# A hybrid attention, Fourier and feed-forward layer on one core: attention's tiles placed in another order, the first feed-forward weights split into attention's buffers, and the start of the second sequence issued in another order

## The chip, the cores and the metric

The kernel runs on one core of a Trainium2 chip. The metric is the time of one execution on the device in microseconds (us), the median of several runs. The core has a tensor engine for matmuls (PE, with its weight loads listed apart as PEld), a vector engine (DVE), a scalar engine (ACT), GpSimd (POOL), a sync engine that issues DMAs (SP), two on-chip memories (SBUF, and PSUM with eight banks, into which PE writes) and 16 DMA engines. Each engine takes its instructions in the order of its own queue, and an instruction that has to wait holds up those behind it.

## The reference

One encoder layer for two sequences of 1024 rows of width 1024, all in float32, with a conditioning vector of their own each. `g_final` is the final norm's gain.

```python
def layer(x, c, ...):
    sh1, sc1, ga1, sh2, sc2, ga2 = split(silu(c) @ w_ada + b_ada, 6)
    h = rmsnorm(x, g_mix) * (1 + sc1) + sh1
    q_lat, kv_lat, k_pe, f_in = split(h @ w_in)
    y_mla = mla_group(...)        # attention with low-rank q and k/v, 4 heads
    y_four = fourier_group(...)   # real part of a 2-D Fourier transform, mixed by group
    x = x + ga1 * (concat(y_mla, y_four) @ w_out)
    h2 = rmsnorm(x, g_ffn) * (1 + sc2) + sh2
    return x + ga2 * ((silu(h2 @ w_gate) * (h2 @ w_up)) @ w_down)
# both sequences go through layer(), then rmsnorm(x, g_final)
```

## The kernel before, in words

**Precision.** Every large matmul is done as three: an operand is split into a high part (a cast on ACT, line L62) and a low part (a subtraction on DVE, L63, which needs the cast), and `mm3` (L78 to L80) adds high x high, high x low and low x high into one PSUM bank. `split(hi, lo, src)` makes such a pair and keeps the two instructions in `here["a"]` and `here["v"]`.

**Stages.** One after the other: input projections; the Fourier part; attention (two sequences of four blocks of four heads, two tiles of 128 rows each: 64 items `k`); the output projection, which runs some items behind attention; the feed-forward's up stage (gate and up) and down stage for sequence 1 (`s == 0` in the code), then for sequence 2 (`s == 1`).

**Attention's tiles.** The pool `e` ("p3e", left side of SBUF) holds what attention reads: the query weights `wq_h` and `wq_l`, two small buffers `hv`, the rotation tables `rc` and `rs`, the keys `lat0`, the query tiles `qsk`, `qa`, `qp`, the latents `ql`, the values `ckv` and the gates `gah`. `stage3_loads` creates them, and tiles lie in the order of their first creation; `q_tiles` creates `qsk`, `qa` and `qp` ahead of `ql` and `ckv`, and an empty tile of 32 bytes ("phase") follows. The pool `w` ("p3", right side) holds `p` (softmax results), `lat1` and the flipped results `pt`. `scores` reads `qa`, `qp` and the keys; `flip_p` transposes and splits `p` into `pt` one item later; `values` multiplies `pt` with `ckv` three items later, and its split goes into the tiles `o0` and `o1` of the pool `tl` ("p4").

**From attention to the feed-forward.** The pool `w` of the feed-forward ("p5") starts at the address at which `e` started, and its tiles (H20, X0, X1, H21, H30, H31, H41, H00, H01, H50 and so on, 8 KB each) lie again in order of creation. A tile can be written as soon as the last reader of every older tile under it is done. `prep_h` loads and splits the seven combinations of the activations that the feed-forward multiplies (a fast matrix product with 7 in place of 8 block products), two half tiles at each `next(prep)`. The first two are ordered behind the last split of `flip_p`; the sums of the first weights (`w0`, four subtractions on DVE) are ordered behind the split of the last `values`; some of norm2 and of the residual adds (L883) are ordered behind the splits (`first(...)`). The last four output projections of sequence 2 (`out_proj(1, 3, ...)`) close the pool `tl`; the pool "p5b" (`wh`, `wl`, `val`) then takes its place.

**The up stage.** For each of 22 weight columns `n` seven products, `step(0)` to `step(6)`, each of twelve matmuls into the banks x, y, z. `combos(n + 1)` loads the next weights (`rgu`) and forms their four sums (`sums_w`, L135) on POOL; after each product one of the next seven weight tiles is split (`hl`). After product 0, ACT copies x into `p1` (L1351); product 2 accumulates further on x. After product 1, DVE adds y and `p1` into `u2` (L138); product 3 accumulates further on y. In the same way the adds after products 3, 4 and 5.

**Row steps.** The down stage's last result is finished row tile by row tile (`rows_out`): a product with the gate (L1467), an add, a square on ACT (L1469), a reciprocal root on POOL (L105 to L110), two scalings on DVE (L1478) and two stores by SP (L1484). For sequence 1 these seven steps stand in the list `pending` and are issued in the first iterations of sequence 2's up stage, two in each: one behind the copy of `p1` and one behind the Silu after product 2, by `behind()` ordered behind the last split on ACT and on DVE.

**What sets the order.** The program's text does not fix the queues. A planner walks through it with estimated durations and takes for each engine the earliest instruction of the program that is ready at that moment. `tc.issue_after(i)` puts every instruction of the block on `i`'s engine behind `i`; it is an order of issue only.

## Time and profile before

| | us |
|---|---|
| median of three runs | 2081.8 |
| lowest, highest | 2078.99, 2082.57 |
| the profiled execution | 2080.45 |
| its span, first to last instruction | 2078.6 |
| mean granted clock of PE | 0.987 |

| stretch of the span, us | what runs |
|---|---|
| 0 to 238 | input projections |
| 238 to 331 | Fourier part |
| 331 to 784 | attention and output projections |
| 784 to 1427 | feed-forward of sequence 1 |
| 1427 to 2079 | feed-forward of sequence 2 |

A row of a profile names a line of the kernel, an engine, an operation and the tiles that it writes and reads (out<-in). In the timeline the first column is the start in us from the span's start, the second the length, and a bracket gives how long the engine stood idle before and what ended that. In the list of waits a row gives who waited, for whom, the total in us, the number of times and the longest. The windows view gives for each stretch the busy time of each engine with the number of its instructions, then the granted clock of PE as a share of full speed, the DMA's share and its rate. Matmuls overlap, so the length of one (0.39 us for 512 columns) is more than the distance between two starts.

### The profile page before, as it was taken

To read this page: it belongs to the slowest core of one execution; us is meant where nothing else is said; L and a number is where in the kernel's file an instruction comes from. 1 tells how busy PE (TensorE), PEld (TensorE's weight loads), DVE (VectorE), ACT (ScalarE), POOL (GpSimd) and SP (SyncE) were. 2 spreads that over 40 slices of the span, in tenths; PEclk is the share of its full clock that TensorE was granted. 3 is DMA by queue.
4 is the path that set the end of the run, shared out by engine and by line. 5 is a ranking of instruction groups with operands and counts; after the bars stand their busy time and mean duration, and the time that the engine had idled before them with its cause. 6 is when DMAs were issued, how large, how long until landed. Compare 5 with 4: busy or idle time off the path is not lost. (4 is left out here: it accounts for less than half of the span.)

```text
span 2078.6 us, 28790 instructions
## 1 busy us (share of the span) xinstructions
PE 2008.3 (97%) x10044; PEld 1667.0 (80%) x10044; DVE 1413.0 (68%) x2089; ACT 903.1 (43%) x1765; POOL 837.3 (40%) x1034
## 2 busy tenths in 40 slices
PE   5899999999999999999999999999999999999997
PEld 2788877888888877888888888877788888888876
DVE  2757757766676768887778776777765565567684
ACT  2666535555565545333333356453333333336441
POOL 1455203111312314888778610335544454420142
PEclk7999999999999999999999999999999999999999
DMA  9586774544543456555555587664332232258672
GB/s 372 191 252 198 230 273 176 132 102 90 149 122 112 155 195 208 176 194 183 192 187 190 165 277 265 212 233 158 136 116 99 89 127 101 78 183 281 221 232 90
DMA packets 182943, 371.30 MB, mean 179 GB/s; under 512 B 19021, under 2 KB 58317, under 8 KB 179725
## 3 DMA queue, kind: packets, MB, share of 16 engines
q1 hardware_dynamic: 163660, 309.80, 44.6%
q0 software_dynamic: 19136, 59.65, 9.5%
q8 instruction: 79, 1.29, 0.3%
q14 instruction: 68, 0.55, 0.1%
HBM read 257.38 MB, written 120.39 MB: 182 GB/s over the span
## 5 line engine op out<-in xcount | busy, mean ns | idle before, releaser
L78 PE MATMUL bank<-H,wh 128*128 128x512 f32 x1232 | 482.2, 392 | 9.7 <-DVE val L138 5.0
L80 PE MATMUL bank<-H,wl 128*128 128x512 f32 x1232 | 481.4, 391 | 1.4 <-DVE wl L63 1.4
L79 PE MATMUL bank<-H,wh 128*128 128x512 f32 x1232 | 481.9, 391 | 0.4 <-DVE H L63 0.4
L138 DVE TENSOR_TENSOR val<-bank,val 128x512 f32<-128x512 f32 x244 | 166.8, 688 | 182.6 <-PE bank L80 179.4
L78 PEld LDWEIGHTS bank<-H,wh 128*128 128x128 f32 x1232 | 232.7, 189 | 60.6 <-DVE val L138 6.1
L80 PEld LDWEIGHTS bank<-H,wl 128*128 128x128 f32 x1232 | 232.7, 189 | 50.5 <-DVE wl L63 1.9
L79 PEld LDWEIGHTS bank<-H,wh 128*128 128x128 f32 x1232 | 232.6, 189 | 49.0 <-DVE H L63 0.8
L63 DVE TENSOR_TENSOR wl<-draw,wh 128x512 fp32r<-128x512 f32 x286 | 201.2, 738 | 87.8 <-ACT wh L62 86.1
L62 ACT CAST wh<-draw 128x512 fp32r<-128x512 f32 x286 | 168.9, 620 | 159.3 <-PE bank L79 81.0
L79 PE MATMUL bank<-wl,wh 128*128 128x512 f32 x572 | 223.9, 391 | 1.9 <-DVE wl L63 1.9
L138 POOL TENSOR_TENSOR val<-val 128x512 f32<-128x512 f32 x58 | 82.9, 1437 | 352.1 <-DVE val L1452 189.4
L78 PE MATMUL bank<-wh 128*128 128x512 f32 x572 | 222.7, 389 | 0.2 <-ACT wh L62 0.2
L80 PE MATMUL bank<-wh,wl 128*128 128x512 f32 x572 | 222.7, 389 | 0.0
L62 ACT CAST wh<-rgu 128x512 fp32r<-128x512 f32 x172 | 107.0, 622 | 261.3 <-PE bank L79 207.3
L62 ACT CAST wh<-val 128x512 fp32r<-128x512 f32 x133 | 82.3, 622 | 270.0 <-PE bank L79 245.1
L63 DVE TENSOR_TENSOR wl<-val,wh 128x512 fp32r<-128x512 f32 x133 | 143.1, 1078 | 68.4 <-ACT wh L62 68.2
L63 DVE TENSOR_TENSOR wl<-rgu,wh 128x512 fp32r<-128x512 f32 x172 | 165.8, 964 | 4.3 <-ACT wh L62 4.3
L135 POOL TENSOR_TENSOR val<-rgu 128x512 f32<-128x512 f32 x84 | 120.3, 1432 | 117.3 <-DMA rgu<-in_wgu_dram 108.3
L79 PEld LDWEIGHTS bank<-wl,wh 128*128 128x128 f32 x572 | 107.3, 188 | 27.8 <-DVE wl L63 5.7
L78 PEld LDWEIGHTS bank<-wh 128*128 128x128 f32 x572 | 107.4, 188 | 23.1 <-ACT wh L62 0.7
L80 PEld LDWEIGHTS bank<-wh,wl 128*128 128x128 f32 x572 | 107.4, 188 | 22.0
L950 DVE TENSOR_REDUCE mx<-ps_s 128x1 f32<-128x1024 f32 x64 | 78.2, 1222 | 62.3 <-PE ps_s L945 61.9
(362 smaller groups left out, 4107.2 us busy)
## 6 DMA issues: line engine op xcount, KB each, us to landing
rgu<-in_wgu_dram SPq DMA_DIRECT2D x86, 512.0 KB
draw<-s_d SPq DMA_DIRECT2D x143, 256.0 KB
s_d<-val POOLq DMA_DIRECT2D x88, 256.0 KB, 4.0
draw<-t_d SPq DMA_DIRECT2D x88, 256.0 KB
s_d<-val SPq DMA_DIRECT2D x66, 256.0 KB
draw<-in_w_down_dram SPq DMA_DIRECT2D x55, 256.0 KB
wada<-in_w_ada_dram SPq DMA_DIRECT2D x13, 1024.0 KB
xt<-in_x_dram SPq DMA_DIRECT2D x16, 512.0 KB
```

The source lines that it names most:

```text
L62: here["a"] = nc.scalar.copy(hi, src).ins
L63: here["v"] = nc.vector.tensor_tensor(out=lo, in0=src, in1=rd(hi), op=ALU.subtract).ins
L78: nc.tensor.matmul(out, lh, rh, start=first, stop=False, skip_group_check=cont)
L79: nc.tensor.matmul(out, lh, rl, start=False, stop=False, skip_group_check=cont)
L80: nc.tensor.matmul(out, ll, rh, start=False, stop=last, skip_group_check=cont)
L135: return eng.tensor_tensor(out=out, in0=x, in1=y, op=ALU.subtract).ins
L138: eng.tensor_tensor(out=out, in0=x, in1=y, op=ALU.add)
L950: nc.vector.tensor_reduce(out=mx, in_=ps, axis=AX.X, op=ALU.max)
```

## The change

- **Attention's pools.** `q_tiles` is gone. `stage3_loads` creates `qsk`, then `ql` and the values' tiles, then `qa`; `qp` is created at its first use, after `ckv`. The empty tile of 32 bytes is left out. In "p3" an empty tile of 32 bytes is created in front of `pt` and one of 480 bytes behind it.
- **First weights.** The first two weight tiles of sequence 1's up stage are split in the third of the last four output projections, into a tile each of the tags `o0` and `o1` of the pool `tl` (high and low parts). The up stage reads them from there, and splits the third tile on as before.
- **First sums of sequence 2.** `combos` forms the sums of iteration 0's and iteration 1's weights of sequence 2 on DVE.
- **The copy and the second split.** In both sequences the split after product 1 is ordered on ACT behind the copy of `p1`.
- **Row steps.** The pending steps are issued behind the adds after products 1 and 3, on DVE's queue alone, in place of the two places above. `add` returns its instruction for that.

```diff
     def add(out, x, y, eng):
-        eng.tensor_tensor(out=out, in0=x, in1=y, op=ALU.add)
+        return eng.tensor_tensor(out=out, in0=x, in1=y, op=ALU.add).ins
...
-    def q_tiles():
-        sk_tile()
-        qa_tiles()
-        qp_tile()
...
         lat = [e.tile([P, 2, N], F32R, tag=f"lat0{i}", name=f"lat0{i}") for i in range(2)]
-        q_tiles()
-        e.tile([P, 8], F32, name="phase")
+        sk_tile()
         load_q(0, 0)
...
             split(wq_h[:, c, 0:512], wq_l[:, c, 0:512], wqr[:, 0:512])
+        qa_tiles()
         nc.sync.dma_start(rc, a["ropec"])
...
         def flip_p(s, b, h, u):
             p = S.pop(("p", s, b, h, u))
+            if (s, b, h, u) == (0, 0, 0, 0):
+                w.tile([P, 8], F32, name="phase_pt")
             if u == 0:
                 S["pt", s, b, h] = [w.tile([P, 8, 2, P], F32R, tag=f"pt{k}", name=f"pt{k}", bufs=2) for k in range(2)]
+            if (s, b, h, u) == (0, 0, 0, 0):
+                w.tile([P, 120], F32, name="phase_l")
...
             if n == 1:
                 norm3(0)
+            if n == 2:
+                fw = [tl.tile([P, 2, 512], F32R, tag=f"o{i}", name=f"fw{i}", bufs=3) for i in range(2)]
+                for i in range(2):
+                    split(fw[0][:, i, :], fw[1][:, i, :], w0[i])
...
-                return sums_w([...], lambda i: val(), nc.gpsimd)
+                return sums_w([...], lambda i: val(), nc.vector if n == 0 or (s == 1 and n == 1) else nc.gpsimd)
...
             if s == 0:
-                wts = [hl(w0[i]) for i in range(2)]
+                wts = [(fw[0][:, i, :], fw[1][:, i, :]) for i in range(2)]
+                fw = None
...
                     elif src is not None:
-                        nxt.append(hl(src[j]))
+                        with ExitStack() as after:
+                            if j == 1:
+                                after.enter_context(tc.issue_after(here["p1"]))
+                            nxt.append(hl(src[j]))
...
                 p1 = val()
-                nc.scalar.copy(p1, x)
-                if pending:
-                    with behind():
-                        pending.pop(0)()
+                here["p1"] = nc.scalar.copy(p1, x).ins
                 step(1, y, 5, True)
                 u2 = val()
-                add(u2, y, p1, nc.vector)
+                here["u"] = add(u2, y, p1, nc.vector)
+                if pending:
+                    with tc.issue_after(here["u"]):
+                        pending.pop(0)()
                 step(2, x, 1, False)
                 sg = val()
                 nc.scalar.activation(sg, x, AF.Silu)
-                if pending:
-                    with behind():
-                        pending.pop(0)()
                 step(3, y, 6, False)
                 u3 = val()
-                add(u3, y, p1, nc.vector)
+                here["u"] = add(u3, y, p1, nc.vector)
+                if pending:
+                    with tc.issue_after(here["u"]):
+                        pending.pop(0)()
```

More of the change, by code (lines that the diff above doesn't have):

```diff
@@ L1245, in combos @@
                     nc.sync.dma_start(r[:, i, :], a["wgu"][i, f])
-                return sums_w([r[:, 0, :512], r[:, 0, 512:], r[:, 1, :512], r[:, 1, 512:]], lambda i: val(), nc.gpsimd)
+                return sums_w([r[:, 0, :512], r[:, 0, 512:], r[:, 1, :512], r[:, 1, 512:]], lambda i: val(), nc.vector if n == 0 or (s == 1 and n == 1) else nc.gpsimd)
             def comb_h(s, c):
```

## The prediction

> **What bounds the kernel now.** I read the page first (busy time by engine), then who the tensor engine (PE) waited for in three stretches, then the timeline round each long wait.

> ```profile
> PE 2008.3 (97%) x10044; PEld 1667.0 (80%) x10044; DVE 1413.0 (68%) x2089; ACT 903.1 (43%) x1765; POOL 837.3 (40%) x1034
> ```

> The change removes no matmul, so at most the 70.3 us of the span (2078.6 less 2008.3) in which PE stands still can go, and with them the time in which it runs slowly after standing still. Who it waited for from 745 to 860 us (attention's end and the feed-forward's start) and from 1420 to 1500 (sequence 2's start), in total us, times, longest:

> ```profile
> PE gb L78 <- DVE x L883: 4.0, 1, 4.0
> PE bank L78 <- DVE val L138: 2.3, 2, 2.1
> PE bank L80 <- DVE wl L63: 1.4, 1, 1.4
> PE bank L78 <- ACT val L1351: 1.3, 1, 1.3
> ...
> PE bank L78 <- ACT wh L62: 0.3, 1, 0.3
> ```

> ```profile
> PE bank L78 <- ACT val L1351: 3.1, 1, 3.1
> PE bank L78 <- DVE val L138: 2.8, 1, 2.8
> ```

> The windows view, cut at the moments when the granted clock falls; columns: stretch, length, PE busy (matmuls), weight loads, DVE, ACT, POOL, then PE clock:

> ```profile
> 765.80:769.20 3.40, 3.40 (x9) 2.63 (x9) 2.41 (x5) 0.81 (x1) 0.64 (x4) 0.50 0.92 303
> 799.90:803.30 3.40, 3.40 (x10) 2.65 (x9) 3.40 (x5) 0.00 (x0) 0.00 (x0) 0.50 0.00 0
> 838.60:842.00 3.40, 3.40 (x15) 2.83 (x16) 2.37 (x3) 1.04 (x3) 3.08 (x4) 1.00 0.05 19
> 1434.80:1441.60 6.80, 5.73 (x14) 4.47 (x15) 6.10 (x9) 2.67 (x6) 2.30 (x3) 0.50 0.43 155
> 1482.60:1486.00 3.40, 3.40 (x9) 2.62 (x9) 3.40 (x3) 0.00 (x0) 3.24 (x3) 0.50 0.01 4
> ```

> After waits of 4.0, 2.1, 3.1 and 2.8 us the clock is 0.50 for 3.4 us (6.8 once); after the one of 1.3 it stays at 1.00. So a long wait costs itself and half of the PE time at half clock: 1.7 us, and 2.9 (half of 5.73) at 1434.8. A 512-column matmul takes 3.40/15 = 0.227 us at full clock, a block of twelve 2.72.

> [...]

> **The change part by part**

> *Attention's pool.* In KB from the pool's start, tiles lie in order of first use: wq 0-12, hv, rc, rs to 20, lat0 20-36, qsk 36-40, then before qa 40-46, qp 46-54, ql 54-62, ckv 62-70, gah 70-72; after ql 40-48, ckv 48-56, qa 56-62, qp 62-70, gah. The feed-forward's pool starts at the same address: H30 32-40, H31 40-48, H41 48-56, H00 56-64, H01 64-72. So H00 and H01, the first split activations, lie before on ql and ckv, and after on qa, qp and gah. ckv is read until attention's last value product; qa and qp only until its last scores. H41 (the sums of the first weights) gets ckv instead, but those sums are already ordered behind that product's split. H31 gets ql in place of qa and half of qp, so SP issues its loads some steps earlier; nothing waits for them. ACT, then DVE:

> ```profile
> 753.23 0.37 ACT L62 CAST o0b<-gb 128x256 fp32r<-128x256 f32 x1 [1.61 <-PE gb L80]
> 761.42 1.99 ACT L62 CAST H<-H 128x1024 fp32r<-128x1024 f32 x2 [7.82 <-PE gb L79]
> ```

> ```profile
> 762.50 2.36 DVE L63 TENSOR_TENSOR H<-H,H 128x1024 fp32r<-128x1024 f32 x2 [5.84 <-ACT H L62]
> 764.78 0.68 DVE L883 TENSOR_TENSOR x<-x,gb 128x512 f32<-128x512 f32 x1
> ```

> ACT stands at the cast of H for 7.8 us until PE has done the value product (761.4); DVE stands 5.8 behind it; the next output projection's residual add (L883) is queued behind both, and PE's bank behind that add: the wait of 4.0. After, both halves of the split (1.99 and 2.36) fit into ACT's and DVE's idle time from 753 on. Gone: 4.0 + 1.7. Late next: norm2 of the last of these rows, which PE's transposes need.

> ```profile
> 767.73 0.68 DVE L135 TENSOR_TENSOR H<-rgu 128x512 f32<-128x512 f32 x1
> ...
> 770.51 0.68 DVE L883 TENSOR_TENSOR x<-x,gb 128x512 f32<-128x512 f32 x1
> ...
> 775.33 0.75 DVE L896 TENSOR_SCALAR xn<-x,rs_r 128x1024 f32<-128x1024 f32 x1 [1.27 <-POOL rs_r L110]
> ```

> Value product ends 761.4, its split 0.37 + 0.42 with hand-overs 762.3, four weight sums (767.73 to 770.5, 2.8) 765.1, the add 765.8, then as in the trace 4.9 from the add's end (771.2) to the scaled row's (776.1): 770.7. PE has three blocks (8.2) until 769.6. It waits 1.1, where the trace has 0.4 at this place: I take 0.8 back. **Gain 4.9**; bounds 3 (the chain 2 later) and 5.7.

> The two empty tiles (32 and 480 bytes) and the 32 bytes taken out move pt, ql and ckv by small offsets. No row shows an offset's price; two rows of the value products, one shape on differently placed tiles:

> ```profile
> L78 PE MATMUL gb<-pt,ckv 128*128 128x256 f32 x256 | 73.7, 288 | 0.0
> ...
> L79 PE MATMUL gb<-pt,ckv 128*128 128x256 f32 x256 | 72.8, 284 | 0.0
> ```

> 0.9 us between them, three such lines: 2.7 either way at most; I take 0. At attention's start nothing is won: in the PE waits from 100 to 745 us no wait names wq or ql.

> *First weights in attention buffers.* The first two weight tiles are split into o0/o1 slots, free since an earlier projection, instead of wh/wl slots that lie on wv and wait for the last projection. Gone: 1.4 (L80 on wl) and 0.3 (wh). The two casts and subtractions move ahead, into DVE's idle time (3.35 before 782.30). Late next is the add at 798.83, the wait of 2.1:

> ```profile
> 782.30 0.75 DVE L1156 TENSOR_SCALAR X<-x,rs_r 128x1024 f32<-128x1024 f32 x1 [3.35 <-POOL rs_r L110]
> ...
> 792.60 1.77 DVE L1156 TENSOR_SCALAR X<-X,rs_r 128x1024 f32<-128x1024 f32 x1 [1.87 <-POOL rs_r L110]
> ...
> 798.83 0.68 DVE L138 TENSOR_TENSOR val<-bank,val 128x512 f32<-128x512 f32 x1
> ```

> Ahead of it DVE waits 1.87 on POOL's reciprocal root of a square on ACT; with two casts fewer (about 0.5 each) that square comes 1.0 sooner. So 1.0 of the 1.7 is kept. **Gain 1.0**; bounds 0 and 5.5 (1.7, and 2.1 + 1.7 if DVE takes the add before the splits of H that stand in front of it).

> *Copy of the first product ahead of the second weight's cast* (j == 1):

> ```profile
> 837.40 0.62 ACT L62 CAST wh<-val 128x512 fp32r<-128x512 f32 x1 [5.10 <-POOL val L135]
> 837.93 0.58 ACT L1351 COPY val<-bank 128x512 f32<-128x512 f32 x1
> ```

> ACT stood 5.1 us at a cast that needs POOL's sum, with the copy behind it; PE's third product accumulates on the bank that is copied. In the new order the copy runs when the first product is done; the cast, late anyway, is needed an iteration later. **Gain 1.2** of the 1.3.

> *Sequence 2's first sums on DVE, same order.* The same cast, here with the copy right behind it, then POOL's sums and DVE's splits:

> ```profile
> 1434.72 0.62 ACT L62 CAST wh<-val 128x512 fp32r<-128x512 f32 x1 [2.69 <-POOL val L135]
> ```

> ```profile
> 1424.20 1.29 POOL L135 TENSOR_TENSOR val<-rgu 128x512 f32<-128x512 f32 x1 [13.35 <-DMA rgu<-in_wgu_dram]
> ...
> 1434.76 1.60 POOL L135 TENSOR_TENSOR val<-rgu,val 128x512 f32<-128x512 f32 x1
> ```

> ```profile
> 1430.08 1.79 DVE L63 TENSOR_TENSOR wl<-rgu,wh 128x512 fp32r<-128x512 f32 x1
> ...
> 1436.83 1.28 DVE L63 TENSOR_TENSOR wl<-rgu,wh 128x512 fp32r<-128x512 f32 x2
> ```

> Eight POOL sums (1424.2 to 1436.4) become eight on DVE at 0.7. While POOL sums, a DVE split takes 1.79; when it stops, 0.64: what the sums add (5.6) the splits give back. From the weights' landing: four sums to 1427.0, eight splits at 0.64 to 1432.1, four sums to 1434.9, then the add that the fourth product needs, done 1435.6; that product is due three blocks after the first, 1435.87 - 3.10 - 5.44 + 8.16 = 1435.5. Gone 3.1 + 2.9, back about 0.4. **Gain 5.6**; bounds 0 and 6.0.

> *Row steps behind the adds:*

> ```profile
> 1473.61 3.62 DVE L1375 TENSOR_TENSOR val<-val 128x512 f32<-128x512 f32 x1
> 1477.16 2.44 DVE L1478 SCALAR_TENSOR_TENSOR val<-val,rs_r,gf 128x512 f32<-128x512 f32 x2
> 1479.52 2.24 DVE L63 TENSOR_TENSOR wl<-val,wh 128x512 fp32r<-128x512 f32 x1
> 1481.68 0.68 DVE L138 TENSOR_TENSOR val<-bank,val 128x512 f32<-128x512 f32 x1
> ```

> Two row scalings (2.44) and a split stand ahead of the add on which PE waits 2.8. After, the scalings are queued behind the add, and the add is ready before the split's cast has come: it runs at 1477.2, ahead of PE's 1479.65. Queued behind it: scalings, split, and the output stores on SP, which nobody waits for. **Gain 4.5**; bounds 0 and 4.5.

> Sum 4.9 + 1.0 + 1.2 + 5.6 + 4.5 = 17.2. The profiled execution took 2080.45 us, the median of the runs is 2081.8: 2063.3 against the one, **2064.6** against the other.

> **The rivals**

> 1. *DVE's queue becomes the bound at sequence 2's start.* POOL starts the third iteration's sums as soon as the buffer is free, while DVE still sums and splits; eight splits at 1.79 in place of 0.64 put the add 9 us back at worst, and the 6.0 come back as a wait on DVE. Time 2070.2. For it: DVE's margin there is below nothing already. Against: the buffer's reload waits for those very splits.
> 2. *The row steps only move the stall.* Behind an add come two scalings (3.4 with POOL beside them, 2.44 half of it), a split 2.24, two row operations 1.4: up to 7.0, where the next add is due after two blocks, 5.4. Four of the seven steps scale: 4 x 1.6, and a half clock of 1.7 where it passes 2: about 9, time 2073.6.
> 3. *The layout doesn't do what it says*: the H split is issued later for another reason (its load, the order on ACT). The 4.9 stay: 2069.5.
> 4. *The half clock stays.* The stretches at 0.50 around 1434.8 and 1482.6 have another cause than the waits in front of them and come anyway: 2.9 + 1.7 fewer, 2069.2. [...] Against: four waits above 2 us are followed by 0.50, and the one of 1.3 is not.
> 5. *Slower.* The order of each engine's queue is planned from waits, and new placements change it in attention, where DVE has little room. There PE's transposes wait on the softmax:

> ```profile
> PE ppt L967 <- DVE nb L951: 1.9, 2, 1.6
> ```

> Twice now, 0.95 each. Once in each of the 32 heads is 30 us: 2094.6. It outweighs the gains from 18 heads on. Against: placements there change by half a KB, and no dependence between attention's instructions does.

> **How the numbers follow.** Forecast 0.53; rival 1 0.14, 2 0.12, 3 0.07, 4 0.03, 5 0.08; 0.03 left for gains that fall away together (within 0.2%). The range reaches from the forecast with the first weights' upper bound and no late row (2059) over rivals 1 to 3 with the half-paid cases, to 2077; outside lie rival 5, the 0.03, some of rival 2 and what falls below 2059. About 0.2%, 4.2 us, is what a measurement of this kernel can tell from no change: below 2077.6 lie the forecast, 1, 3, 4 and three quarters of 2: faster 0.86, same 0.05, slower 0.09.

> **What would show it.** After: no wait of PE on L883 near 761, and ACT's first H cast before 756; no wait of L80 on wl at the first product; both waits on L1351 gone; no half clock near 1432 and 1480; PE busy time smaller by about 6. Wrong would be: a wait on L138 of 2 us or more after 1425, an H cast still ended by a gb matmul, or attention's ppt waits above 10 us in sum.

## The result, and the profile after

The changed kernel takes 2073.06 us (median of 6 runs, 2072.22 to 2074.31), the kernel before 2080.85 (6 runs). The ratio is 0.9965, 95% interval 0.9952 to 0.9978: 7.8 us less by the medians, where 17.2 was forecast. The profiled execution took 2073.43, its span is 2071.7.

The page and the two lists of waits, over the stretches that the prediction read (745 to 860 us, then 1420 to 1500); lines lie 1 to 5 lower in the middle of the file than before (L1155 for L1156, L878 for L883), 7 higher at its end:

```profile
PE 2001.2 (97%) x10044; PEld 1661.8 (80%) x10044; DVE 1417.9 (68%) x2097; ACT 902.8 (44%) x1765; POOL 831.7 (40%) x1026
```

```profile
PE bank L79 <- DVE H L63: 9.3, 1, 9.3
PE bank L78 <- ACT H L62: 1.5, 1, 1.5
PE pht L1162 <- DVE xn L891: 1.2, 1, 1.2
PE bank L78 <- DVE val L138: 0.7, 1, 0.7
```

```profile
PE bank L78 <- DVE val L138: 2.9, 3, 1.1
```

Every wait that the change was to remove is gone: the residual add (4.0), the first weights (1.4), the copy (1.3 and 3.1), the add at 1482 (2.8). PE's busy time fell by 7.1. But a wait of 9.3 us that before did not have stands at the start of the feed-forward. The windows view round it (columns as in the prediction), in steps of 3.41 us; the clock is 0.50 from 788.16 to 798.40:

```profile
784.75:788.16 3.41, 0.00 (x0) 0.00 (x0) 0.28 (x1) 3.15 (x5) 0.10 (x1) 1.00 0.40 162
788.16:791.58 3.42, 0.00 (x0) 0.00 (x0) 3.42 (x5) 0.00 (x0) 2.25 (x2) 0.50 0.10 37
791.58:794.99 3.41, 1.09 (x3) 0.91 (x4) 3.41 (x5) 0.00 (x0) 0.00 (x0) 0.50 0.43 115
794.99:798.40 3.41, 3.41 (x10) 2.67 (x9) 3.41 (x5) 1.04 (x1) 0.00 (x0) 0.50 1.00 380
```

PE stands still to 793.9, and the 4.5 us of work after it run at half clock (2.2 lost). In the first stretch DVE works 0.28 of 3.41 us, so DVE itself is waiting. Its timeline, and POOL's and SP's DMA issues:

```profile
777.48 1.22 DVE L63 TENSOR_TENSOR H<-H,H 128x1024 fp32r<-128x1024 f32 x1
778.61 0.68 DVE L878 TENSOR_TENSOR X<-X,gb 128x512 f32<-128x512 f32 x1
787.88 0.75 DVE L1155 TENSOR_SCALAR X<-X,rs_r 128x1024 f32<-128x1024 f32 x1 [8.59 <-DMA x_d<-X]
788.55 1.75 DVE L63 TENSOR_TENSOR wl<-rgu,wh 128x512 fp32r<-128x512 f32 x1
...
792.63 2.35 DVE L63 TENSOR_TENSOR H<-H,H 128x1024 fp32r<-128x1024 f32 x2
```

```profile
779.59 0.65 POOL L1149 DMA_DIRECT2D x_d<-X  x1 [2.82 <-DVE X L878]
...
782.41 0.19 POOL L110 TENSOR_TENSOR rs_r<-rs_w,rs_y 128x1 f32<-128x1 f32 x1
```

```profile
777.59 1.77 SPq L1244 DMA_DIRECT2D val<-in_wgu_dram  x4
779.46 0.38 SPq L1266 DMA_DIRECT2D tdb<-in_w_down_dram  x1
```

L1155 is the second row tile's scaling in `norm3`. It writes X over X, and X is just being stored to DRAM (L1149): the reciprocal root is there at 782.6, but DVE stands 8.6 us until the store has landed. Behind it in DVE's queue are five weight splits and the split of the second activations (H, 792.63), which PE's third product needs. Before, the same scaling stood behind seven weight splits, and when they were done the store, issued at 786.8, had nearly landed (791.4): the scaling waited 1.9 for the root. The last of those splits and the store's issue before:

```profile
790.05 0.69 DVE L63 TENSOR_TENSOR wl<-rgu,wh 128x512 fp32r<-128x512 f32 x1
```

```profile
786.82 0.65 POOL L1150 DMA_DIRECT2D x_d<-X  x1 [4.55 <-DVE X L883]
```

The store's row in the list of DMA issues (KB, us to landing), first before, then after:

```profile
x_d<-X POOLq DMA_DIRECT2D x1, 512.0 KB, 4.6
```

```profile
x_d<-X POOLq DMA_DIRECT2D x1, 512.0 KB, 8.2
```

To compare parts I use two marks that every trace has: from PE's restart after its wait of 0.5 us near 706 (on `qa`) to its restart after the one of 0.9 to 1.0 at the end of sequence 1's down stage (near 1410), here "the middle", and from there to the restart after the last wait above 0.3 on `wl` near 2005, "sequence 2". They leave out the first 240 us, whose length differs by up to 2.4 us from run to run. A mark is one trace's; a ratio is of several runs. The three restarts, before and after:

```profile
706.40 0.50 PE L943 MATMUL ps_s<-lat,qa 128*128 128x512 f32 x1 [0.50 <-DVE qa L63]
1413.56 0.50 PE L79 MATMUL bank<-wl,wh 128*128 128x512 f32 x1 [0.91 <-DVE wl L63]
2012.82 0.50 PE L79 MATMUL bank<-wl,wh 128*128 128x512 f32 x1 [0.40 <-DVE wl L63]
```

```profile
705.28 0.50 PE L938 MATMUL ps_s<-lat,qa 128*128 128x512 f32 x1 [0.48 <-DVE qa L63]
1413.19 0.50 PE L79 MATMUL bank<-wl,wh 128*128 128x512 f32 x1 [0.93 <-DVE wl L63]
2005.72 0.50 PE L79 MATMUL bank<-wl,wh 128*128 128x512 f32 x1 [0.41 <-DVE wl L63]
```

| profiled execution, us | middle | sequence 2 |
|---|---|---|
| before | 707.2 | 599.3 |
| after | 707.9 | 592.5 |

The middle, where 7.1 was to be won by layout, first weights and copy, won nothing; sequence 2 won 6.7 of 10.1.

### The profile page after: what moved, and what is told of

Its sections match the earlier page's. It is cut to its first block, busy times and chain, and to the rows that moved or that the text cites. A ratio compares the mean times of both kernels' runs of the same rounds, so it can differ in the third digit from the quotient of the medians.

```text
span 2071.7 us, 28756 instructions
## 1 busy us (share of the span) xinstructions
PE 2001.2 (97%) x10044; PEld 1661.8 (80%) x10044; DVE 1417.9 (68%) x2097; ACT 902.8 (44%) x1765; POOL 831.7 (40%) x1026
## 3 DMA queue, kind: packets, MB, share of 16 engines
q8 instruction: 79, 1.29, 0.3%
## 4 chain that ended last, share of the span: by engine, by line
PE 52%; DVE 4%; DMA 2%; issue 1%; POOL 1%; ACT 1%; SPq 0%; DVEq 0%; ACTq 0%; POOLq 0%
PE bank L79 18%; PE bank L78 18%; PE bank L80 17%; DVE wl L63 2%; DVE val L138 1%; DMA val<-x_d 1%; DMA draw<-s_d 1%; POOL val L138 1%; DMA draw<-t_d 1%; ACT wh L62 0%; DVE val L1485 0%; POOL rs_y L106 0%; DMA draw<-in_w_down_dram 0%; DVE val L1459 0%; SPq L1444 0%
## 5 line engine op out<-in xcount | busy, mean ns | idle before, releaser
L79 PE MATMUL bank<-H,wh 128*128 128x512 f32 x1224 | 477.4, 390 | 9.3 <-DVE H L63 9.3
L78 PE MATMUL bank<-H,wh 128*128 128x512 f32 x1224 | 477.9, 390 | 5.5 <-DVE val L138 4.1
L80 PE MATMUL bank<-H,wl 128*128 128x512 f32 x1224 | 476.8, 390 | 0.0
L138 DVE TENSOR_TENSOR val<-bank,val 128x512 f32<-128x512 f32 x244 | 166.7, 688 | 166.8 <-PE bank L80 162.6
L79 PEld LDWEIGHTS bank<-H,wh 128*128 128x128 f32 x1224 | 230.3, 188 | 57.2 <-DVE H L63 9.6
L78 PEld LDWEIGHTS bank<-H,wh 128*128 128x128 f32 x1224 | 230.3, 188 | 56.2 <-DVE val L138 6.8
L80 PEld LDWEIGHTS bank<-H,wl 128*128 128x128 f32 x1224 | 230.2, 188 | 48.3
L63 DVE TENSOR_TENSOR wl<-draw,wh 128x512 fp32r<-128x512 f32 x286 | 201.0, 737 | 88.5 <-ACT wh L62 87.2
L62 ACT CAST wh<-draw 128x512 fp32r<-128x512 f32 x286 | 168.6, 620 | 157.3 <-PE bank L79 80.6
L79 PE MATMUL bank<-wl,wh 128*128 128x512 f32 x572 | 223.8, 391 | 2.5 <-DVE wl L63 2.4
L138 POOL TENSOR_TENSOR val<-val 128x512 f32<-128x512 f32 x58 | 83.3, 1444 | 351.0 <-DVE val L1459 186.4
L78 PE MATMUL bank<-wh 128*128 128x512 f32 x572 | 222.7, 389 | 0.0
L80 PE MATMUL bank<-wh,wl 128*128 128x512 f32 x572 | 222.7, 389 | 0.0
L62 ACT CAST wh<-rgu 128x512 fp32r<-128x512 f32 x171 | 106.3, 622 | 248.8 <-PE bank L79 192.8
L63 DVE TENSOR_TENSOR wl<-val,wh 128x512 fp32r<-128x512 f32 x133 | 143.3, 1079 | 74.0 <-ACT wh L62 73.9
L63 DVE TENSOR_TENSOR wl<-rgu,wh 128x512 fp32r<-128x512 f32 x171 | 163.8, 958 | 2.5 <-ACT wh L62 2.4
L62 ACT CAST wh<-val 128x512 fp32r<-128x512 f32 x133 | 82.3, 622 | 183.9 <-PE bank L79 162.5
L135 POOL TENSOR_TENSOR val<-rgu 128x512 f32<-128x512 f32 x80 | 112.6, 1407 | 103.6 <-DMA rgu<-in_wgu_dram 99.9
L79 PEld LDWEIGHTS bank<-wl,wh 128*128 128x128 f32 x572 | 107.3, 188 | 28.9 <-DVE wl L63 6.7
L78 PEld LDWEIGHTS bank<-wh 128*128 128x128 f32 x572 | 107.4, 188 | 22.8 <-ACT wh L62 0.4
L80 PEld LDWEIGHTS bank<-wh,wl 128*128 128x128 f32 x572 | 107.4, 188 | 21.9
```

The costliest lines, as they stand in the source:

```text
L62: here["a"] = nc.scalar.copy(hi, src).ins
L63: here["v"] = nc.vector.tensor_tensor(out=lo, in0=src, in1=rd(hi), op=ALU.subtract).ins
L78: nc.tensor.matmul(out, lh, rh, start=first, stop=False, skip_group_check=cont)
L79: nc.tensor.matmul(out, lh, rl, start=False, stop=False, skip_group_check=cont)
L80: nc.tensor.matmul(out, ll, rh, start=False, stop=last, skip_group_check=cont)
L135: return eng.tensor_tensor(out=out, in0=x, in1=y, op=ALU.subtract).ins
```

## The experiments

Each ratio is against runs of the kernel before on the same chip, with its 95% interval. Theory: part B (the first weights) put the scaling ahead of the splits, and there it waits for the store. Rival: the feed-forward's start is bound by the arrival of activations and casts, and no order on DVE changes that. In the expectations the parts are lettered: A layout, B first weights, C copy, D sums, E row steps.

**First weights undone, in the changed kernel.**

```diff
-            if n == 2:
-                fw = [...]
-                for i in range(2):
-                    split(fw[0][:, i, :], fw[1][:, i, :], w0[i])
...
-                wts = [(fw[0][:, i, :], fw[1][:, i, :]) for i in range(2)]
-                fw = None
+                wts = [hl(w0[i]) for i in range(2)]
```

> The changed kernel with one part undone: the first two weight tiles of sequence 1 are split in the feed-forward's own buffers again, as before the change; layout, copy order, sums and row steps stay changed. Theory: in the changed kernel PE's wait of 9.3 us at 793.9 (and half clock behind it) comes from DVE, which stood 8.5 us, to 787.8, at the second norm3 scaling, because that scaling overwrites the tile X in place and so waits for X's store to DRAM; part B put that scaling ahead of the five splits of the weights. Without part B it stands behind seven splits, where the kernel before had it. So PE has no wait over 2.5 us from 776 to 800, the start of the feed-forward keeps the layout's 4.9 us, and the time is 2080.85 less 4.9 (layout), 1.2 (copy), 6.0 (sums) and 1.6 (row steps, 4.5 less the three new waits of 2.85): 2067, 6 us under the changed kernel. Rival: the start of the feed-forward is bound by the arrival of the activations and casts, which no order on DVE changes, and whatever the layout wins is waited off before 800: 2073, as the changed kernel.

2066.75 us, ratio 0.9943 (0.9929 to 0.9958); middle 700.6, sequence 2 592.6. DVE's timeline there, the last of seven splits and the scaling:

```profile
784.90 0.68 DVE L63 TENSOR_TENSOR wl<-rgu,wh 128x512 fp32r<-128x512 f32 x1
787.46 1.77 DVE L1155 TENSOR_SCALAR X<-X,rs_r 128x1024 f32<-128x1024 f32 x1 [1.87 <-POOL rs_r L110]
```

The order of before is back, and with it 7.3 us of the middle; by the ratios (0.9965 and 0.9943) the whole is 4.6 us shorter. The rival's 2073 is out.

**First weights alone, in the kernel before** (the same edit the other way).

> The kernel before with part B alone: the first two weight tiles split into the o0 and o1 buffers. Theory (part B puts the second norm3 scaling ahead of the other weight splits on DVE, and DVE stands there until X's store has landed): a PE wait of 8 us or more with half clock at the start of the feed-forward; the waits that part B was to remove (1.4, 0.3, 2.1 and a half clock of 1.7) go. Net slower than before by 5 to 7 us, ratio 1.0025 to 1.0035. Rival (the long wait arises only together with the new layout, which brings the last projections forward): the forecast's step B, 1.0 us faster, ratio 0.9995.

2086.92 us, ratio 1.0035 (1.0021 to 1.0049); middle 714.0, 6.8 more than before. PE's waits from 745 to 860 us there, the longest two, and DVE's scaling:

```profile
PE bank L79 <- DVE H L63: 8.9, 1, 8.9
PE gb L78 <- DVE x L883: 4.0, 1, 4.0
```

```profile
794.40 1.75 DVE L1156 TENSOR_SCALAR X<-X,rs_r 128x1024 f32<-128x1024 f32 x1 [8.25 <-DMA x_d<-X]
```

So part B makes the kernel slower by itself, with or without the new layout.

**The norm behind the first weights' splits.**

```diff
-                            norm3(1, S.pop("jk3").bitcast(BF16))
+                            with behind():
+                                norm3(1, S.pop("jk3").bitcast(BF16))
```

> The changed kernel with the second norm3 (square on ACT, scaling on DVE) ordered behind the last cast and the last subtraction of the first weights; the scaling stays in place and stays ahead of the splits of the second activations. Theory (DVE stands at the scaling until X's store has landed, about 787.8): the five weight splits are then done while it waits, so the splits of the activations end 0.75 + 1.2 after 787.8, PE resumes near 789.8 in place of 793.9, still with half clock behind it: 4 us faster than the changed kernel, 2069. Rival (arrival of the activations and casts): no gain, 2073.

2066.28 us, ratio 0.9941 (0.9925 to 0.9957). The wait of 9.3 became 3.2 and 2.4, though the half clock of 10.2 us stayed:

```profile
778.97 0.69 DVE L63 TENSOR_TENSOR wl<-rgu,wh 128x512 fp32r<-128x512 f32 x1
782.30 0.69 DVE L63 TENSOR_TENSOR wl<-H,wh 128x512 fp32r<-128x512 f32 x1 [2.65 <-ACT H L62]
...
786.99 0.75 DVE L1155 TENSOR_SCALAR X<-X,rs_r 128x1024 f32<-128x1024 f32 x1 [2.19 <-POOL tdb L135]
787.66 4.62 DVE L63 TENSOR_TENSOR H<-H,H 128x1024 fp32r<-128x1024 f32 x4
```

The splits are done while the store runs (it landed at 786.9; the releaser in the row had long been done). More was won than the 4 us expected: the square on ACT moved behind the weight casts as well, and PE's wait of 1.5 on ACT is gone. The 2.65 at the second split lasts until the second product ends: that `wl` buffer lies on the `o0` buffer which part B fills and both first products read.

**A tile of its own for the scaled rows**, order as in the changed kernel.

```diff
+            if u == 1:
+                S["xn", 1, 3, u] = S["gf"]
             nc.vector.tensor_scalar(out=S["xn", 1, 3, u], in0=x2, ...)
```

> The changed kernel with the order on DVE left as it is, but the second norm3 scaling writes into another tile (that of the final norm's gain, loaded afterwards) and so waits for nothing but POOL's reciprocal root (782.6), and not for the store. Theory: scaling 783.4, five weight splits to 786.8, first activation split 788.0: PE waits 1.5 and then about 3.3 in place of 9.3, and its clock drops for half of the time or not at all: 6 to 7 us faster than the changed kernel, 2066.5. Rival (arrival of the activations and casts): no gain, 2073.

2067.81 us, ratio 0.9948 (0.9933 to 0.9963); PE's waits 1.5 and 4.0.

```profile
783.73 0.75 DVE L1157 TENSOR_SCALAR gf<-X,rs_r 128x1024 f32<-128x1024 f32 x1 [3.35 <-POOL rs_r L110]
```

The scaling now runs when the root is there, though the store lands 3.8 us later (787.5): it is the overwriting that costs.

**The store ahead of the loads**, order on PE, ACT and DVE as in the changed kernel.

```diff
-            nc.gpsimd.dma_start(x2_d[1][...], x2)
+            here["st"] = (nc.gpsimd, nc.sync)[u].dma_start(x2_d[1][...], x2).ins
...
-                        nc.sync.dma_start(t, a["wgu"][...])
+                        with tc.issue_after(here["st"]):
+                            nc.sync.dma_start(t, a["wgu"][...])
...
-                nc.sync.dma_start(b1, ...)
+                with tc.issue_after(here["st"]):
+                    nc.sync.dma_start(b1, ...)
...
+                norm3(1, S.pop("jk3").bitcast(BF16))
                 wts += [hl(w0[i]) for i in (2, 3)]
...
-                            norm3(1, S.pop("jk3").bitcast(BF16))
```

> The changed kernel with the order on PE, ACT and DVE as it is; only X's store is issued by SP ahead of the five loads (four of the second weights, one for the down stage) that were issued from 777.6 to 779.5, instead of by POOL right behind them. Theory (the store is queued behind these 1.5 MB): it lands 3.1 to 4.6 us after its issue, as the two stores before it, so near 783.5 in place of 787.75; DVE goes on 4 us sooner, PE's wait of 9.3 becomes 5 and the half clock behind it stays: 4 us faster than the changed kernel, ratio 0.9945. Rival (the store is slow for another reason): it lands 7 us or more after its issue, no gain, ratio 0.9965.

2066.77 us, ratio 0.9936 (0.9922 to 0.9949); PE's waits 1.4 and 3.0.

```profile
777.94 0.33 SPq L1149 DMA_DIRECT2D x_d<-X  x1
778.36 2.21 SPq L1245 DMA_DIRECT2D val<-in_wgu_dram  x4
```

```profile
777.23 0.68 DVE L878 TENSOR_TENSOR X<-X,gb 128x512 f32<-128x512 f32 x1
781.23 0.75 DVE L1155 TENSOR_SCALAR X<-X,rs_r 128x1024 f32<-128x1024 f32 x1 [3.32 <-ACT wh L62]
```

```profile
781.00 0.19 POOL L110 TENSOR_TENSOR rs_r<-rs_w,rs_y 128x1 f32<-128x1 f32 x1
```

The scaling starts 3.3 us after the store's issue, as soon as the root is there (781.2), so the store has landed by then. The 8.2 us came with the 1.5 MB of loads (four of 256 KB, one of 512) issued in the 2 us before it. SP in place of POOL as the issuing engine was changed with it; the two stores of rows that POOL issued just before in the changed kernel (764.9 and 773.5), with no such loads ahead of them, took 3.0 and 3.1 us.

**The norm behind the first add**, and the same with both first weight tiles in `o1` buffers:

```diff
-                            norm3(1, S.pop("jk3").bitcast(BF16))
...
                 here["u"] = add(u2, y, p1, nc.vector)
+                if "jk3" in S:
+                    with tc.issue_after(here["a"]), tc.issue_after(here["u"]):
+                        norm3(1, S.pop("jk3").bitcast(BF16))
```

> The changed kernel with the second norm3 moved: its store, square and scaling come behind the first add of the feed-forward (after the splits of two activations on DVE and their casts on ACT); the scaling stays in place. Theory: nothing on DVE stands ahead of the weight and activation splits, the casts on ACT begin some 3 us sooner, PE waits under 2 us in sum there and keeps its clock: 9.3 + 2.2 (half of 4.5 us of PE work at half clock) less 2, 9.5 us faster than the changed kernel, 2063.5. Rival (arrival of the activations and casts): PE waits for the last activations instead, loaded into X, before 800: no less than 2070.

2066.52 us, ratio 0.9946 (0.9929 to 0.9963). From the feed-forward's start PE ran to 790.1 without a wait, then waited 4.8 for a weight split. That is more than the theory's 2 us; the rival had a wait before 800, but for activations and at a higher price.

> The changed kernel with the second norm3 moved behind the first add, as in the run of the late norm, and in addition both first weight tiles split into the o1 buffers, which no weight buffer of the feed-forward lies on. In the run of the late norm DVE stood 2.65 us at the second weight split until the second product was done, the load into X was issued at 783.5 behind the last of those splits, and PE waited 4.8 us at 794.9 on splits that DVE does after X's. Theory (the overlap with o0 is what delays X): X is loaded 2.6 us sooner, that wait falls to about 2.2 and the half clock behind it goes or not, 3 us faster than that run, ratio 0.9930 (0.992 to 0.994). Rival (the start is bound by DVE's work as a whole, 17 splits and adds from 777 to 794): no gain, ratio 0.9945.

2070.12 us, ratio 0.9951 (0.9938 to 0.9963). The load into X was issued 4.9 us after the first product's start in place of 8.0, and PE still waited 4.4: my theory of the overlap fell. DVE's row before that wait's end:

```profile
793.31 0.75 DVE L1155 TENSOR_SCALAR X<-X,rs_r 128x1024 f32<-128x1024 f32 x1 [0.91 <-POOL rs_r L110]
793.98 2.35 DVE L63 TENSOR_TENSOR H<-X,H 128x1024 fp32r<-128x1024 f32 x2
```

DVE's queue, with the scaling in it again ahead of X's splits, sets the end.

**Norm behind the splits, own tile, `o1` buffers, all three.**

> The changed kernel with three edits at the feed-forward's start: the second norm3 ordered behind the first weights' splits, its scaling written into a tile of its own (so it waits for no store), and both first weight tiles split into the o1 buffers (in the run with the norm ordered behind, the second weight split on DVE stood 2.65 us until the second product was done: the weight tiles behind it lie on o0's buffer, and the load into X waits for those splits). Theory: no wait of DVE above 2 us from 777 to 790, X loaded 2.6 us sooner than there; of that run's PE waits (3.2 and 2.4) and 10 us of half clock some 3 us go: 2063, ratio 0.9925 (0.9915 to 0.9935). Rival (the start is then bound by the activations' arrival): as that run, 2066, ratio 0.994.

2066.85 us, ratio 0.9934 (0.9919 to 0.9949): the rival's value. The 2.65 is gone, and PE waits 4.1 on an add that stands behind four activation splits on DVE.

**The layout alone, in the kernel before.**

> The kernel before with attention's pools laid out anew and nothing else changed. The order on DVE there keeps the second norm3 scaling behind the seven weight splits. Theory (the forecast's step A): the wait of 4.0 near 761 and its half clock go, about 0.8 comes back at the transposes, no wait above 2.5 us after 776: 4.9 us faster, ratio 0.9976. Rival (the start of the feed-forward is bound by arrival, so the time won is waited off before 800): ratio 0.999 or more.

2074.72 us, ratio 0.9976 (0.9966 to 0.9987): 5.0 us; middle 702.8.

**Sequence 2: sums alone, row steps alone, sums and copy, in the kernel before.** The edits are those of the change.

> The kernel before with sequence 2's first two sets of sums on DVE and nothing else changed. Theory (the forecast's step): the wait of 3.1 at 1435.9 and its half clock go, 5.6 us faster, ratio 0.9973; the wait of 2.8 at 1482 stays. Rival (DVE's queue becomes the bound): a wait on DVE's add after 1432 takes its place, ratio 0.999 or more.

2076.59 us, ratio 0.9982 (0.9969 to 0.9994). On the copy a wait of 1.7 stayed, and 1.2 and 1.0 on adds (1420 to 1500 us):

```profile
PE bank L78 <- DVE val L138: 2.2, 2, 1.2
PE bank L78 <- ACT val L1351: 1.7, 1, 1.7
```

> The kernel before with the row steps issued behind the adds and nothing else changed. Theory after the result (the changed kernel has three waits of 0.81, 1.07 and 0.97 on adds there in place of one of 2.76 with a half clock): 4.5 less 2.85, 1.6 us faster, ratio 0.9992, the wait of 3.1 at 1435.9 unchanged. Rival 1 (the forecast's step E, the three small waits belong to the sums on DVE): 4.5 us faster, 0.9978, no wait above 0.5 from 1440 to 1490. Rival 2 (the steps behind adds lengthen the waits to over 2 us): slower than before.

2078.92 us, ratio 0.9992 (0.9982 to 1.0001). The three waits are the row steps' own. DVE's timeline ahead of the second:

```profile
1476.35 0.69 DVE L138 TENSOR_TENSOR val<-bank,val 128x512 f32<-128x512 f32 x1 [1.28 <-PE bank L80]
1476.96 3.99 DVE L1478 SCALAR_TENSOR_TENSOR val<-val,rs_r,gf 128x512 f32<-128x512 f32 x2
1480.87 2.25 DVE L63 TENSOR_TENSOR wl<-rgu,wh 128x512 fp32r<-128x512 f32 x1
1483.05 1.77 DVE L63 TENSOR_TENSOR wl<-val,wh 128x512 fp32r<-128x512 f32 x1
1484.74 0.68 DVE L138 TENSOR_TENSOR val<-bank,val 128x512 f32<-128x512 f32 x1
```

Two scalings and two splits, 8.0 us while POOL sums, stand between an add and the next.

> The kernel before with sequence 2's first sums on DVE and the copy of the first product ahead of the second weight's cast, in both sequences. In the run with the sums alone a wait of 1.69 on that copy stayed at 1434 and the wait of 1.3 at 838 with it. Theory (forecast's steps C and D together): both go, and PE runs without a wait over 0.6 us from 1415 to 1450: 5.6 + 1.2 = 6.8 us faster, ratio 0.9967. Rival (behind the copy another wait on DVE's add stands, as the forecast's first rival has it): 1 to 2 us of wait after 1434 stay, 4.5 us faster, 0.9978.

2077.03 us, ratio 0.9983 (0.9974 to 0.9993): no more than the sums alone. The copy's waits are gone, but 2.8 on the add at 1479 with its half clock is back, which the sums alone had at 1.2 and 1.0. The middle is 708.4 against 707.4 with the sums alone: a wait of 1.9 on an add at 823 has half clock behind it.

**The copy's order undone, first weights undone too.**

> The changed kernel with the first weights undone and, besides, the copy of the first product left in its old order against the second weight's cast. Theory after the runs (the forecast's step C, 1.2 us, is paid back: where the copy comes first the wait on the add before it grows from 0.5 to 1.6, and alone with the sums it brought nothing): within 0.5 us at 815 to 835, and in sequence 2 a wait of 1 to 1.7 on the copy comes back, so 1 to 2 us slower than with the copy first, ratio 0.995. Rival (step C as forecast): a wait of 1.3 near 833 and one of 1.7 in sequence 2 come back with nothing given: 3 us slower, 0.9957.

2071.08 us, ratio 0.9954 (0.9938 to 0.9969), against 0.9943 with the copy first. The waits of 1.3 at 833 and 1.6 at 1429 come back, and the add's wait at 815 is 1.8 without it too: nothing was paid back, the rival was right. In the marks the copy's order is worth 1.5 us in the middle (702.1 against 700.6) and 3.1 in sequence 2 (595.7 against 592.6).

**One row step in each iteration**, on four kernels, first on that with the norm behind the first add and both first weight tiles in `o1` buffers:

```diff
                 here["u"] = add(u3, y, p1, nc.vector)
-                if pending:
-                    with tc.issue_after(here["u"]):
-                        pending.pop(0)()
```

> The same, and the row steps of sequence 1's last rows one in each iteration of sequence 2 (behind the add after product 1 alone) in place of two. Theory (the waits of 0.8, 1.1 and 1.0 on adds from 1455 to 1485 are DVE's queue, two row steps on top of seven splits in each iteration): these 2.85 us go, ratio 0.0014 under the run without it. Rival (four banks are held by the row tiles for two iterations longer, and PE waits on banks): no gain or slower.

2066.51 us, ratio 0.9936 (0.9924 to 0.9949), 3.6 us under the run without it (0.9951) on the same chip.

> The changed kernel with the first weights undone and the row steps one in each iteration of sequence 2 in place of two. Theory (the three waits of 0.81, 1.08 and 0.95 on adds there are DVE's queue): they go, 2.8 us less than with the first weights undone alone (0.9943), ratio 0.9929, 2066 or less. Rival (the row steps only move on): ratio 0.9943.

2064.89 us, ratio 0.9925 (0.9912 to 0.9937); sequence 2 590.2. In place of three waits (2.8 in sum) one of 0.3 and one of 0.7. It is the shortest median of the study, 8 us under the changed kernel.

> The run of the clear path (0.9934) with the row steps one in each iteration. Theory: as above 0.0014 less, ratio 0.992. Rival: 0.9934.

2066.28 us, ratio 0.9926 (0.9913 to 0.9940): 0.0008 under 0.9934, where 0.0014 was expected; the intervals overlap.

> The changed kernel, all its parts kept, with X's store issued by SP ahead of the loads and the row steps one in each iteration of sequence 2. Theory (the two edits add up: 0.9936 with the store first, 2.85 us of waits less): ratio 0.992, about 2064 to 2065, no better than the same row steps with the first weights undone (0.9925), since PE still waits 1.5 and 3.0 us for the second activations with half clock behind it. Rival (part B then gives its forecast 1.0 us and more): 0.9915 or less.

2065.17 us, ratio 0.9932 (0.9919 to 0.9946), against 0.9936 with the store first alone, 0.992 expected, and 0.9925 without part B: with both mechanisms out of the way part B is worth nothing that can be measured.

## Why the prediction was right or wrong

| part | forecast | alone, by ratio | in the marks |
|---|---|---|---|
| layout | 4.9 | 5.0 | 4.4 (middle) |
| first weights | 1.0 | -7.3; -4.6 on top of the others | -6.8 alone, -7.3 on top of the others |
| copy | 1.2 | none; 2.3 with first weights undone | 1.5 (middle), 3.1 (sequence 2), first weights undone |
| sums | 5.6 | 3.7 | 4.9 (sequence 2) |
| row steps | 4.5 | 1.7 | 2.4 (sequence 2) |
| copy, sums and row steps in sequence 2 | 10.1 | | 6.7; 9.0 with one step in each iteration |

**Layout: right**, in place and size. ACT's first H cast ran at 752.4, the add's wait is gone, the transposes wait 1.2 where 1.1 was worked out; rival 3 is out. Two slips in its working change the gain by 0.1 at most: H31 gets a quarter of qp, not half, and 1.1 less 0.4 is 0.7, where 0.8 was taken back.

**First weights: this step failed.** It was to win 1.0 us and cost 4.6 (by ratio, on top of the others) to 7.3 (alone): 5.6 to 8.3 of the 9.4 us that the forecast was off. It said "Ahead of it DVE waits 1.87 on POOL's reciprocal root of a square on ACT; with two casts fewer that square comes 1.0 sooner. So 1.0 of the 1.7 is kept." The waits named did go. But the step kept the scaling at its old place in DVE's queue, where the change moved it ahead of the five weight splits that were left; and it priced the scaling by the one releaser that the row named. The row it quoted, X<-X, shows the second: the overwritten tile waits for its readers, and one reader is a DMA, the store (8.59 us of waiting for it in the changed kernel). In the trace of before the store landed at 791.4 and the root came at 792.6, so the store was 1.2 us from being the later one. Its bounds, 0 and 5.5, had no loss in them. Why the planner put the scaling ahead when two splits were taken away isn't shown by any run; that it did, in both kernels with part B, and in none without, is.

**Copy: right in the changed kernel, not by itself.** With the first weights undone it won 1.5 in the middle, where 1.2 was forecast, and 3.1 in sequence 2, which the forecast had under the sums; by ratio 2.3 in all, with intervals that overlap. On the kernel before with the sums on DVE it won nothing (0.9983 against 0.9982): its own waits went, but waits on adds grew and two of them, 1.9 and 2.8, had half clock behind them.

**Sums: the mechanism right, the size too large alone.** The 3.1 became 1.7, not 0, without the copy's new order; both together left 1.0 on the add behind it (sums and copy), a small form of rival 1.

**Row steps: mis-sized.** The 2.8 and its half clock went, and three waits of 2.9 in sum came. Rival 2 had this mechanism (behind an add come two scalings and a split) and 1.6 apiece; the two scalings took 4.0 where it had 3.4, yet the waits were 0.8 to 1.1 and none had half clock behind it. Its price of about 9 was high by its own terms (4 x 1.6 and 1.7 are 8.1). The sum went by the add that runs ahead, and not by what the steps then put in front of the next one. With half as many steps in each iteration the waits are gone.

**Half clock: right in the main, too simple in going by the wait's length.** With the waits near 1432 and 1480 the half clock behind them went (none from 798.40 to 2064.7 us in the trace after), so rival 4 is out; but a wait of 2.5 us left the clock at 1.00 with the row steps alone, where 2.1 had cost half clock before (last section). **Attention** kept its time: from the start of the Fourier part (238) to the mark near 706 before took 468.2 us, after 467.1, and runs with the old layout 466.9 to 468.2; rival 5 is out.

What stays open is what holds the feed-forward's start after the store is out of the way: six different repairs all gave 0.993 to 0.995, each with 4 to 6 us of PE's waits from 776 to 860 and 6.8 to 10.2 us of half clock behind them. The longest of these waits is on DVE each time: on the split of the second activations (norm behind the splits, own tile, store first), on a weight split (norm behind the first add, with and without `o1`) or on an add (all three).

## What to carry to other kernels

When a queue's order is planned anew, ask for each instruction with a long list of followers what else it waits for than the releaser that the trace names, and how near the runner-up was: the in-place scaling here waited 8.6 us for a DMA store that reads its tile, where 1.2 us had parted store and root before. A store that something waits for belongs ahead of bulk loads, not behind them (here it took 8.2 us to land behind 1.5 MB of loads, and at most 3.3 ahead of them). Work put into an engine's idle time is free only as long as the order around it stays (the first weights alone cost 7.3 us); before counting a gain, bound it below nothing where the order is not yours.

## What the runs showed of the hardware that was not expected

```profile
1431.40:1434.82 3.42, 2.07 (x10) 1.37 (x8) 3.42 (x3) 0.72 (x2) 3.23 (x3) 1.00 0.00 0
1434.82:1438.23 3.41, 2.25 (x10) 1.88 (x11) 3.41 (x5) 1.62 (x3) 1.60 (x1) 1.00 0.00 0
```

```profile
1431.38:1434.80 3.42, 1.39 (x7) 0.81 (x5) 3.42 (x3) 0.73 (x3) 3.25 (x3) 1.00 0.00 0
1434.80:1438.21 3.41, 2.34 (x6) 1.85 (x7) 3.41 (x5) 1.02 (x2) 1.56 (x1) 0.50 0.00 0
```

From 235 to 2040 us of all 19 traces, the 25 steps at full clock with 2.0 us or more idle were all followed by half clock, those with 1.6 or less never, and between them both occur. In the traces before and after, the steps with 2.02, 2.10, 2.76, 3.14 and 3.41 us idle were followed by 0.50, and all with 1.61 or less by 1.00. So waits of one length cost half clock or not by their place on the grid, and the grid lies differently in each trace: in the run with the first weights alone a wait of 2.9 that ended at 1442.4 cost none, and one of 2.9 that ended at 1488.4 cost 3.4 us of it.
